# A two-layer latent diffusion backbone on one core: statistics of the Fourier mixer on TensorE, and five changes to the order of small steps

## The chip, the cores and the metric

The kernel runs on one core of a Trainium2 chip. A core has five engines that run side by side, each with its own instruction queue: TensorE (PE in the profile; its weight loads are PEld), VectorE (DVE), ScalarE (ACT), GpSimd (POOL) and SyncE (SP), which here issues most DMAs. The metric is the device time of one execution in microseconds; below, the time of a kernel is the median of its runs.

## What is computed

Two layers over 512 tokens of 1024 channels, all in fp32. The first layer's mixer is attention, the second's is a Fourier mix; each layer ends with a gated feed-forward net (FFN) with a width-3 convolution over tokens. Cut to what matters here:

```python
for i in range(2):
    sh1, sc1, g1, sh2, sc2, g2 = split(silu(c) @ mod_w[i] + mod_b[i])      # "adaLN"
    h = rms_norm(x, norm_g[i, 0]) * (1 + sc1) + sh1
    if i == 0:
        y = attention_mixers(h, ...)
    else:
        y = real(fft2(h in 4 channel groups)) @ w_f
    x = x + g1 * rms_norm(y, norm_g[i, 1])
    h = rms_norm(x, norm_g[i, 2]) * (1 + sc2) + sh2
    u = conv3(h @ w_up)                       # 2 x 2816 columns: gate and value
    y = (silu(gate) * value) @ w_down
    x = x + g2 * rms_norm(y, norm_g[i, 3])
```

Every rms_norm needs the sum of squares over all 1024 channels of a token.

## The kernel before, in words

Activations lie with channels on the 128 partitions: 8 tiles of 128 channels by 512 tokens, in two halves of 256 tokens. An fp32 operand is split into a high and a low part, and each product is three matmuls (`mm3`, L108 to L110: high times high, high times low, low times high). So each weight tile needs a cast on ACT and a subtraction on DVE (`split`, L144); up to five such pairs are held at a time (`wpair`), and three raw tiles.

A scheduler places the instructions of each engine in an order fixed before the run: an instruction becomes a candidate when its inputs and buffers are ready in the scheduler's own clock, and among candidates the one written first goes first. Three helpers bind the order by hand: `follow(i, j)` puts i behind j on their engine, `in_turn` chains whole steps on PE and DVE, and `fence()` with `held()` keeps weight splits (and the adaLN sums) behind what was written before the fence. `later(n)` makes a step count as written n places later. At run time each engine works through its own queue in order.

The places that the change touches, in order of time:

- **adaLN sums in layer 0's FFN** (`gemv_jobs`, L538 on; from 323 to 632 us). Five vectors of 1024 outputs are made on DVE: eight multiply-adds of 1024 columns into `gacc` (L570, L573), then `gemv_end` sums over partitions by four 32-column matmuls (L615), copies, transposes (L625) and adds the bias. The generator is pumped one step at a time between FFN tiles.
- **The Fourier mix** (`over_tokens`, `cosines`, `sines`, `group`, then the loop over d at the end of that section). For each of 8 output tiles d, an odd part (12 matmuls with B) and an even part (15 matmuls, the first three with N, the rest with A) make `yT[:, d]`: ACT copies the odd part to `qs`, DVE adds for columns 0 to 255 (L1923), ACT copies column 256 (L1926), DVE subtracts for the rest (L1927). ACT squares the tile (L316), POOL adds the squares of d = 1 to 5 into `acc` (L318; L305 writes the first), those of d = 6 and 7 go to TensorE directly, and ACT scales the tile by its gate (L1933). TensorE sums squares over partitions by `stat_add` (L211): four 32-column matmuls of 64 tokens each for a half. DVE also makes the sum and difference of the next `w_f` tile (L1833, L1834) and its low part. Meanwhile POOL issues DMAs that load the second FFN's first four weight tiles and add their low parts to ACT's `wl = -wh` (L1325 to L1335).
- **The second FFN's opening.** Five first up-projections (units) run over half 0, then half 1; `remod` (L351 on) writes the final input of a half, tile by tile, on DVE and ACT. The sixth unit runs half 0, then half 1.
- **Units by seven products.** From f = 8 on in layer 1 (and for ten f in layer 0) an up-projection pair is made by a Strassen-like scheme of seven products of half size (`seven_products`, L1379 on). `seven_inputs` (L1346 on) makes the combined inputs, eight DVE operations of 1024 columns and four casts; for layer 1 it stands ahead of f = 7. Three copies on ACT (L1398, L1400, L1402) take partial products out of PSUM; the later products of the unit write where these copies read. The weights of the next unit are cast on ACT too; the cast of "1", 512 columns, needs only the raw tile's DMA.
- **The last adaLN vector** (`gemv_pair`), pumped at the down-projection tiles that GEMV lists for each group.
- **The end** (L1947 on). Half 1 of the last down-projection ends tile by tile: DVE adds (L1487), ACT squares (POOL adds up five of them, L318; the last three stay apart, L309), ACT scales by the gate (L1949). `sums_all` sums the four squares over partitions (L226), and `rstd_all` makes 1/sqrt by an ACT estimate `r` (L232), `v` = mean + eps (ACT, L233) and three DVE steps (L234 to L236).

## Time and profile before

| what | us |
|---|---|
| median of 3 runs | 1095.69 (1092.93 to 1097.57) |
| the profiled execution, its own time | 1092.73 |
| the profiled span | 1091.0 |

In the profile a line such as "L144 ACT CAST wh<-raw" is one instruction or a group of them: line of the kernel, engine, operation, written tile and read tiles. "[0.59 <-DVE gacc L573]" behind an instruction says that its engine sat idle for 0.59 us before it and which instruction the profile takes to have ended that. Matmuls overlap: a 256-column one is shown 0.28 us long while the next starts 0.11 us after it. The granted TensorE clock was 1.00 in every stretch that was asked for.

### The profile page before, as it was taken

What the parts mean: (1) busy time and instruction counts of PE and PEld (TensorE: products, weight loads), DVE (VectorE), ACT (ScalarE), POOL (GpSimd) and SP (SyncE); (2) the same over time, 40 slices, a digit from 0 to 9 for tenths busy, and PEclk for the clock granted to TensorE, in tenths of its full rate; (3) what the DMA queues carried; (4) which work ended last, traced back from release to release, by engine and by line L of the source; (5) the groups of instructions that cost most, each with busy time, mean ns of one, the idle gap of its engine ahead of it and who ended that gap; (6) DMA issues with size and microseconds to landing.
All of it is one profiled execution on the core that took longest, in us unless ns stands there. A gap on an engine that the chain in (4) does not pass through costs nothing.

```text
span 1091.0 us, 22506 instructions
## 1 busy us (share of the span) xinstructions
PE 1067.9 (98%) x9352; PEld 1006.0 (92%) x9352; DVE 890.3 (82%) x1451; ACT 601.5 (55%) x1060; POOL 112.3 (10%) x119
## 2 busy tenths in 40 slices
PE   9999999999999999999999999999999999999997
PEld 5699888869999999999999999979999999999996
DVE  5788877774679976878999877888998999889855
ACT  4442366675656633552465476767755465556533
POOL 0046122522100000000000020310000000000012
PEclk9999999999999999999999999999999999999999
DMA  9776101175231474426724630842215533323342
GB/s 367 284 261 213 40 1 40 37 270 196 78 156 39 157 261 147 171 88 229 263 84 153 228 108 2 261 126 117 90 38 169 200 107 114 115 86 103 113 149 78
DMA packets 33911, 156.53 MB, mean 143 GB/s; under 512 B 3472, under 2 KB 8208, under 8 KB 22160
## 3 DMA queue, kind: packets, MB, share of 16 engines
q1 hardware_dynamic: 32656, 150.89, 38.6%
q0 software_dynamic: 1152, 4.19, 1.6%
q8 instruction: 73, 1.20, 0.4%
q14 instruction: 30, 0.25, 0.1%
HBM read 148.78 MB, written 6.29 MB: 142 GB/s over the span
## 4 chain that ended last, share of the span: by engine, by line
PE 72%; DVE 16%; ACT 5%; DMA 3%; issue 3%; POOL 0%; DVEq 0%; POOLq 0%; SPq 0%; ACTq 0%
PE mm L108 20%; PE mm L110 19%; PE mm L109 19%; DVE wl L144 4%; PE PT L1123 1%; DVE cv L1462 1%; DVE cv L1464 1%; ACT wh L144 1%; DMA xl<-in_mod_r 1%; PE gm L108 1%; ACT yT L366 1%; PE O L109 1%; PE gm L109 1%; PE gm L110 1%; PE O L108 1%
## 5 line engine op out<-in xcount | busy, mean ns | idle before, releaser
L144 ACT CAST wh<-raw 128x1024 fp32r<-128x1024 f32 (+2 forms) x206 | 189.9, 931 | 150.6 <-PE mm L109 92.3
L108 PE MATMUL mm<-hh,wh 128*128 128x256 f32 x852 | 236.8, 279 | 3.3 <-ACT sq L1400 2.6
L144 DVE TENSOR_TENSOR wl<-raw,wh 128x1024 fp32r<-128x1024 f32 (+2 forms) x206 | 219.7, 1072 | 23.3 <-ACT wh L144 22.4
L110 PE MATMUL mm<-hh,wl 128*128 128x256 f32 x852 | 235.4, 277 | 1.4 <-DVE wl L144 1.4
L109 PE MATMUL mm<-hl,wh 128*128 128x256 f32 x852 | 235.7, 277 | 0.3 <-DVE hl L369 0.3
L108 PEld LDWEIGHTS mm<-hh,wh 128*128 128x128 f32 x852 | 159.7, 188 | 5.7 <-ACT sq L1400 3.0
L110 PEld LDWEIGHTS mm<-hh,wl 128*128 128x128 f32 x852 | 160.1, 188 | 2.4 <-DVE wl L144 2.3
L109 PEld LDWEIGHTS mm<-hl,wh 128*128 128x128 f32 x852 | 159.9, 188 | 0.6 <-DVE hl L369 0.5
L108 PE MATMUL mm<-xh,wh 128*128 128x256 f32 x492 | 136.7, 279 | 0.0
L109 PE MATMUL mm<-xl,wh 128*128 128x256 f32 x492 | 136.3, 277 | 0.0
L110 PE MATMUL mm<-xh,wl 128*128 128x256 f32 x492 | 135.9, 277 | 0.0
L108 PE MATMUL mm<-zh,wh 128*128 128x256 f32 x384 | 106.6, 278 | 0.5 <-ACT sq L1398 0.5
L110 PE MATMUL mm<-zh,wl 128*128 128x256 f32 x384 | 106.2, 276 | 0.0
L109 PE MATMUL mm<-zl,wh 128*128 128x256 f32 x384 | 106.2, 276 | 0.0
L108 PEld LDWEIGHTS mm<-xh,wh 128*128 128x128 f32 x492 | 92.3, 188 | 1.3 <-issue 0.4
L109 PEld LDWEIGHTS mm<-xl,wh 128*128 128x128 f32 x492 | 92.4, 188 | 0.5 <-issue 0.4
L110 PEld LDWEIGHTS mm<-xh,wl 128*128 128x128 f32 x492 | 92.4, 188 | 0.0
L318 POOL TENSOR_TENSOR cv<-cv,sq 128x256 f32<-128x256 f32 x20 | 16.6, 832 | 702.0 <-ACT sq L316 702.0
L108 PEld LDWEIGHTS mm<-zh,wh 128*128 128x128 f32 x384 | 72.1, 188 | 1.1 <-ACT sq L1398 0.9
L110 PEld LDWEIGHTS mm<-zh,wl 128*128 128x128 f32 x384 | 72.2, 188 | 0.0
L109 PEld LDWEIGHTS mm<-zl,wh 128*128 128x128 f32 x384 | 72.1, 188 | 0.0
L1461 ACT ACTIVATE cv<-mm,cols 128x512 f32<-128x512 f32 x59 | 45.7, 776 | 12.8 <-DVE mm L1405 7.9
(472 smaller groups left out, 2789.8 us busy)
## 6 DMA issues: line engine op xcount, KB each, us to landing
raw<-in_w_up SPq DMA_DIRECT2D x42, 1024.0 KB, 5.0
xT<-in_mod_r SPq DMA_DIRECT2D x20, 1024.0 KB, 4.9
raw<-in_w_down SPq DMA_DIRECT2D x32, 384.0 KB, 3.1
raw<-in_mod_p SPq DMA_DIRECT2D x8, 1024.0 KB, 5.0
raw<-in_w_down SPq DMA_DIRECT2D x16, 512.0 KB, 4.8
raw<-in_w_in SPq DMA_DIRECT2D x6, 1024.0 KB, 8.3
yT<-in_mod_r SPq DMA_DIRECT2D x10, 512.0 KB, 5.9
raw<-in_w_out SPq DMA_DIRECT2D x4, 1024.0 KB, 5.8
```

Source lines behind the costliest of these rows:

```text
L108: i = PE.matmul(out, lhsT=ah, rhs=bh, start=start, stop=False, skip_group_check=skip)
L109: PE.matmul(out, lhsT=ah, rhs=bl, start=False, stop=False, skip_group_check=skip)
L110: return i, PE.matmul(out, lhsT=al, rhs=bh, start=False, stop=stop, skip_group_check=skip)
L144: i = S.copy(out=h, in_=src), eng.tensor_tensor(out=l, in0=src, in1=f(h), op=ALU.subtract)
L318: G.tensor_tensor(out=self.acc[:, sl], in0=self.acc[:, sl], in1=sq[:, sl], op=ALU.add)
L366: S.activation(out=yT[:, c, halves[h]], in_=yT[:, c, halves[h]], func=AF.Identity, bias=bm[:, c:c + 1], scale=am[:, c:c + 1])
L1123: PE.transpose(out=pt[:, j * P:(j + 1) * P], in_=Ps[j][:, off:off + P], identity=ident)
L1461: S.activation(out=cv, in_=ps, func=AF.Identity, bias=bc, scale=wc[1])
L1462: V.scalar_tensor_tensor(out=cv[:, 1:], in0=ps[:, :T - 1], scalar=wc[0], in1=cv[:, 1:], op0=ALU.mult, op1=ALU.add)
L1464: V.scalar_tensor_tensor(out=cv[:, :T - 1], in0=ps[:, 1:], scalar=wc[2], in1=cv[:, :T - 1], op0=ALU.mult, op1=ALU.add)
```

## The change

It moves the sums of squares of the Fourier loop from POOL to TensorE (`RowSums`, with `run` behind the even part of d = 2, 4 and 6), fixes the order of that loop's steps on PE, folds column 256 into the DVE addition and puts N last in the even part; takes the last token block's sines ahead of its cosines and lets the fence stand ahead of the last `cosines`; gates of d = 0 to 5 count as written 1000 places later, those of 6 and 7 come by halves behind the last square. In the FFNs: the end of adaLN jobs 2 to 4 comes one pump later, and for jobs 3 and 4 its matmuls are bound behind the PE instruction written last; `gemv_pair` is spread over three groups; `seven_inputs` of layer 1 is written behind f = 7; the sixth unit's two halves are parted by the first half of the next unit, whose gate weights are cast ahead of `remod(1)` and whose value weights stay behind a new fence; the cast of "1" must follow the copy L1402 of the unit before. At the end, the last three gates follow the last square, the sums run in the order sixth tile, seventh, `acc`, eighth, each bound behind the one before, and `v` is made on DVE.

```diff
-GEMV = {0: (0, 5, 7), 1: (0, 2, 4, 6)}
+GEMV = {0: (0, 7), 1: (1, 3, 5), 2: (0, 2)}
+GAP = 2
...
 def rstd_all(ps):
-        S.activation(out=v, in_=ps, func=AF.Identity, bias=eps, scale=1.0 / D)
+        V.tensor_scalar(out=v, in0=ps, scalar1=1.0 / D, scalar2=EPS, op0=ALU.mult, op1=ALU.add)
...
 def sums_all(self, pps, h):
-            stat_all(ps, self.acc[:, halves[h]], True, False)
-            for sq in self.last[h]:
-                j = stat_all(ps, sq[:, halves[h]], False, sq is self.last[h][-1])
+            a, b, c = self.last[h]
+            sq, j = [a, b, self.acc, c], []
+            for i, s in enumerate(sq):
+                j.append(stat_all(ps, s[:, halves[h]], i == 0, s is c))
+                if i:
+                    follow(j[i], j[i - 1])
...
+    class RowSums:
+        def square(self, src, d, hs):
+            if d not in self.sqs:
+                self.sqs[d] = self.sq = mk(cp, [P, T], F32, "sq", 2)
+            sl = slice(hs[0] * HT, (hs[-1] + 1) * HT)
+            self.end = S.activation(out=self.sqs[d][:, sl], in_=src[:, sl], func=AF.Square)
+        def run(self, ds, hs=(0, 1)):
+            for h in hs:
+                for d in ds:
+                    stat_add(self.ps[h], self.sqs[d][:, halves[h]], HT, d == 0, d == KC - 1)
...
 def gemv_jobs(jobs, pps, away=None):
             end = gemv_end(l, v, acc, pps)
-            next(end)
+            if places and job == GAP:
+                yield
+            if places and job > GAP:
+                behind_pe(end)
+            else:
+                next(end)
...
 def seven_weights(l, fi):
-            split(wh, wl, src)
+            c = split(wh, wl, src)[0]
+            if names == "1" and copied:
+                follow(c, copied.pop())
 def seven_products(l, fi, pps, bs):
-        S.copy(out=xs[:, HT:], in_=y[:, HT:])
+        copied.append(S.copy(out=xs[:, HT:], in_=y[:, HT:]))
...
 def ffn(l, xp, ready, pre, mid, gem, plain=None):
+            ahead = up_weights(l, wpair, [FIRST])
+            wa = next(ahead)
             remod(1, *n2, R[1])
+            fence()
+            wa = [wa, next(ahead)]
...
-                for s in halves:
-                    up_mm(ps, w, s)
+                m = [up_mm(ps, w, halves[0])]
+                pa = mk(pps, [P, T], F32, "mm", 6)
+                m += [up_mm(pa, wa[0], halves[0]), up_mm(ps, w, halves[1])]
+                for j in (1, 2):
+                    follow(m[j][0][0], m[j - 1][-1][1])
...
-                if fi == SUMS[l]:
+                if fi == SUMS[l] and fi in SEVEN[l]:
                     bs = seven_inputs(xp)
...
+                    if fi == SUMS[l]:
+                        bs = seven_inputs(xp)
...
 # the Fourier section
+        for g in range(4):
+            in_turn(sines, g, [3])
         for g in range(4):
             in_turn(group, g, [3])
+        fence()
         in_turn(cosines, None, [v[:4] for v in N], [z[:, :, :, P] for z in Z], list(range(TT)), True)
-        fence()
...
-        ys = YStat(wk, 2)
+        turn.pop(mybir.EngineType.DVE)
+        ys = RowSums(pps)
...
-                pump(soon)
+                with later(60):
+                    pump(soon)
...
+            in_turn(odd, d, wh, wl)
+            pp = in_turn(even, d, wh, wl)
+            if d in (2, 4, 6):
+                in_turn(ys.run, [d - 2, d - 1])
+            qs = qq[d % 2]
+            V.tensor_tensor(out=yT[:, d, 0:257], in0=pp[:, 0:257], in1=qs[:, 0:257], op=ALU.add)
             if d == KC - 1:
-                ys.add(pps, yT[:, d, halves[0]], [0])
-            S.copy(out=yT[:, d, 256:257], in_=pp[:, 256:257])
+                in_turn(ys.run, [d - 1])
+                ys.square(yT[:, d, :], d, [0])
+                in_turn(ys.run, [d], [0])
             V.tensor_tensor(out=yT[:, d, 511:256:-1], in0=pp[:, 1:256], in1=qs[:, 1:256], op=ALU.subtract)
+            ys.square(yT[:, d, :], d, [1] if d == KC - 1 else [0, 1])
             if d == KC - 1:
-                ys.add(pps, yT[:, d, halves[1]], [1])
-            else:
-                ys.add(pps, yT[:, d, :], [0, 1])
-            with later(3000 if d == KC - 1 else 0):
-                S.activation(out=yT[:, d, :], in_=yT[:, d, :], func=AF.Copy, scale=der[:, 1, 1, d:d + 1])
+                in_turn(ys.run, [d], [1])
+            if d < 6:
+                with later(1000):
+                    gate(d, slice(0, T))
+        with later(3000):
+            for hs in halves:
+                for d in (6, 7):
+                    follow(gate(d, hs), ys.end)
...
 # the end
-            S.activation(out=yT[:, k, hb], in_=yT[:, k, hb], func=AF.Copy, scale=der[:, 1, 3, k:k + 1])
+            j = S.activation(out=yT[:, k, hb], in_=yT[:, k, hb], func=AF.Copy, scale=der[:, 1, 3, k:k + 1])
+            if k > KC - 4:
+                follow(j, ys.square)
```

The even part now runs A first and N last; `odd` writes the copied odd part into one of two fixed tiles whose column 256 is zero.

More of the change, by code (lines that the diff above doesn't have):

```diff
@@ L308, in add @@
                 sq = mk(self.late, [P, T], F32, "cv%d" % (n % 2), 2)
-                S.activation(out=sq[:, sl], in_=src, func=AF.Square)
+                self.square = S.activation(out=sq[:, sl], in_=src, func=AF.Square)
                 self.last[1].append(sq)
@@ L324, in sums_all @@
             ps = mk(pps, [P, T], F32, "misc", 2)
-            stat_all(ps, self.acc[:, halves[h]], True, False)
-            for sq in self.last[h]:
-                j = stat_all(ps, sq[:, halves[h]], False, sq is self.last[h][-1])
-            return ps, j
+            a, b, c = self.last[h]
[4 more added lines that the diff above has]
+                    follow(j[i], j[i - 1])
+            return ps, j[-1]
         def sums(self, pps, h):
@@ L337, in sums, with __init__ @@
             self.last = {0: [], 1: []}
+            return self.ps[h]
+    class RowSums:
+        def __init__(self, pps):
+            self.ps = [mk(pps, [P, T], F32, "misc", 2) for _ in halves]
+            self.sqs = {}
+        def square(self, src, d, hs):
[7 more added lines that the diff above has]
+                    stat_add(self.ps[h], self.sqs[d][:, halves[h]], HT, d == 0, d == KC - 1)
+        def sums(self, pps, h):
             return self.ps[h]
@@ L559, in gemv_jobs @@
         n = 0
-        for l, v in jobs:
+        for job, (l, v) in enumerate(jobs):
             acc = mk(cp, [P, D], F32, "gacc", 1)
@@ L1358, in seven_inputs @@
         return b
+    copied = []
     def seven_weights(l, fi):
@@ L1627, in ffn @@
                     cc = []
-                    for i, w in enumerate(up_weights(l, wpair, [fi])):
-                        ps = mk(pps, [P, T], F32, "mm", 6)
-                        m = [up_mm(ps, w, s) for s in halves]
-                        follow(m[1][0][0], m[0][-1][1])
+                    given = l and fi == FIRST
+                    for i, w in enumerate(wa if given else up_weights(l, wpair, [fi])):
+                        if given and i == 0:
+                            ps = pa
+                            up_mm(ps, w, halves[1])
+                        else:
+                            ps = mk(pps, [P, T], F32, "mm", 6)
+                            m = [up_mm(ps, w, s) for s in halves]
+                            follow(m[1][0][0], m[0][-1][1])
                         cc.append(conv(fi, i, ps))
+                    if fi == SUMS[l]:
+                        bs = seven_inputs(xp)
                 gated(fi, cc[0], cc[1], f0)
@@ L1822, in group @@
         def group(g, ts):
-            if ts[-1] == TT - 1:
-                sines(g, ts)
             cosines(g, [v[:, g, :] for v in A], [z[:, :, g, 0:P] for z in Z], ts)
@@ L1905, with odd, even, gate @@
         soon = up_weights_dma(1, xp.weights, [0, 1])
-        ys = YStat(wk, 2)
+        turn.pop(mybir.EngineType.DVE)
+        ys = RowSums(pps)
+        qq = [mk(wk, [P, 258], F32, "qs%d" % i) for i in range(2)]
+        for q in qq:
+            V.memset(q[:, 256:257], 0.0)
+        def odd(d, wh, wl):
+            pq = mk(pps, [P, T], F32, "mm", 6)
+            for g in range(4):
+                mm3(pq[:, :256], wh[:, 1, g, :], wl[:, 1, g, :], B[0][:, g, :], B[1][:, g, :], g == 0, g == 3)
+            S.copy(out=qq[d % 2][:, :256], in_=pq[:, :256])
+        def even(d, wh, wl):
+            pp = mk(pps, [P, T], F32, "mm", 6)
+            for g in range(4):
+                mm3(pp[:, :M1], wh[:, 0, g, :], wl[:, 0, g, :], A[0][:, g, :], A[1][:, g, :], g == 0, False)
+            mm3(pp[:, :M1], nyh[:, d * P:(d + 1) * P], nyl[:, d * P:(d + 1) * P], N[0], N[1], False, True)
+            return pp
+        def gate(d, hs):
+            return S.activation(out=yT[:, d, hs], in_=yT[:, d, hs], func=AF.Copy, scale=der[:, 1, 1, d:d + 1])
         for d in range(KC):
```

10 lines of the change are left out of this document (removed).

## The prediction

> **What bounds the kernel now.** I read the page first, then the chain of waits that ended last, then each engine's waits, then a table by stretches of time, then the timeline around every stop of TensorE.
>
> ```profile
> span 1091.0 us, 22506 instructions
> ```
>
> ```profile
> PE 1067.9 (98%) x9352; PEld 1006.0 (92%) x9352; DVE 890.3 (82%) x1451; ACT 601.5 (55%) x1060; POOL 112.3 (10%) x119
> ```
>
> The profiled execution took 1092.73 us in all, 1.73 beyond this span; the median of the runs is 1095.69, 2.96 above it. TensorE is the bound, and what can be won is its stops. The next view gives stretches: start and end, length, busy time of PE, PEld, DVE, ACT and POOL, then clock and DMA share.
>
> ```profile
> 520.00:580.00 60.00, 59.25 (x519) 58.08 (x518) 58.42 (x72) 32.29 (x51) 0.00 (x0) 1.00 0.48 169
> 690.00:720.00 30.00, 27.38 (x249) 26.16 (x247) 25.04 (x40) 22.28 (x44) 13.41 (x13) 1.00 0.99 297
> 755.00:824.00 69.00, 68.01 (x595) 67.56 (x594) 67.80 (x103) 47.29 (x71) 0.00 (x0) 1.00 0.19 63
> 849.00:927.00 78.00, 75.44 (x664) 74.51 (x663) 75.52 (x97) 45.20 (x72) 0.00 (x0) 1.00 0.38 129
> ```
>
> In three of them DVE is as full as PE (58.42 of 60, 67.80 of 69, 75.52 of 78 us): a stop removed there can come back as a wait for DVE. In the Fourier loop (690 to 720) the DMA engines are full instead (0.99). Now TensorE's stops that the change touches, from the timeline; the bracket is the idle time before the instruction and what ended it.
>
> ```profile
> 513.04 0.64 PE L615 MATMUL misc<-gacc,ones 128*32 128x256 f32 x8 [0.59 <-DVE gacc L573]
> 544.33 0.39 PE L110 MATMUL mm<-hh,wl 128*128 128x256 f32 x1 [0.41 <-DVE wl L144]
> 575.12 0.38 PE L110 MATMUL mm<-hh,wl 128*128 128x256 f32 x1 [0.31 <-DVE wl L144]
> 691.23 0.39 PE L109 MATMUL mm<-B,wh 128*128 128x256 f32 x1 [0.39 <-DVE B L144]
> 692.79 0.39 PE L108 MATMUL mm<-N,wh 128*128 128x258 f32 x1 [0.72 <-ACT N L144]
> 714.57 0.38 PE L108 MATMUL mm<-B,wh 128*128 128x256 f32 x1 [0.43 <-ACT yT L1926]
> 715.83 0.38 PE L110 MATMUL mm<-B,wl 128*128 128x256 f32 x1 [0.76 <-DVE wl L144]
> 762.16 0.38 PE L109 MATMUL mm<-hl,wh 128*128 128x256 f32 x1 [0.34 <-DVE hl L369]
> 808.98 0.38 PE L110 MATMUL mm<-hh,wl 128*128 128x256 f32 x1 [0.64 <-DVE wl L144]
> 866.35 0.39 PE L108 MATMUL mm<-hh,wh 128*128 128x256 f32 x1 [1.56 <-ACT sq L1400]
> 881.22 0.38 PE L108 MATMUL mm<-hh,wh 128*128 128x256 f32 x1 [0.99 <-ACT sq L1400]
> ```
>
> A stop costs more than its bracket. The rows below (of the second FFN's opening, where squares are already summed on TensorE) show why, and price such a sum as well.
>
> ```profile
> 729.36 0.28 PE L109 MATMUL mm<-hl,xh 128*128 128x258 f32 x1
> 729.48 0.28 PE L110 MATMUL mm<-hh,xl 128*128 128x258 f32 x1
> 729.69 0.43 PE L211 MATMUL mm<-yT,ones 128*32 128x64 f32 x16
> 730.05 0.39 PE L108 MATMUL mm<-hh,xh 128*128 128x258 f32 x1
> 730.28 0.29 PE L109 MATMUL mm<-hl,xh 128*128 128x258 f32 x1
> ```
>
> Matmuls start 0.12 us apart but are drawn 0.28 long, so 0.16 of a stop hides under the drawn end; and the first one after it holds up the next by 0.23 instead of 0.12. So a stop costs its bracket plus about 0.28.
>
> **The change, part by part.**
>
> *adaLN sums later.* PE waits 0.59 + 0.28 = 0.87 us at 513 for `gacc`; a pump later the sum is long made. Two further stops follow, 0.41 and 0.31 plus 0.28 each, 1.28 together, where weights' low parts come late from a full DVE. Of job 3 the last two multiply-adds, 1.28 us each by the row below, move behind them.
>
> ```profile
> L573 DVE SCALAR_TENSOR_TENSOR gacc<-xT,cols,gacc x35: 1272/1276/1287, 372.9 to 613.0; 128x1024 f32<-128x1024 f32 x35
> ```
>
> They are 2.56 us of DVE against 1.28 of stops, but job 3 also begins a pump later, and if DVE idles meanwhile, that wastes what was won. Between all and nothing I take half: -0.6. The restore of `xT` and job 4's sums move by one pump too, where PE sees no stop. Part: -1.5 (-0.9 to -2.2).
>
> *Fourier loop, entry.* The stops at 691.23 and 692.79 cost 0.67 and 1.00. With all sines first, B is split early and the first goes. For N:
>
> ```profile
> 692.77 0.41 DVE L144 TENSOR_TENSOR N<-mm,N 4x258 fp32r<-4x258 f32 x1 [0.60 <-ACT N L144]
> ```
>
> N's low part is done at 693.18, last of a chain on DVE that the change doesn't shorten. Its use moves behind 12 matmuls with A, 12 x 0.12 = 1.44 us, but PE gets there 0.67 earlier: wanted at 691.92 - 0.67 + 1.44 = 692.69, one matmul later for the low part. About 0.5 us of waiting stays. Entry: -1.67 + 0.5.
>
> *Fourier loop, POOL.* The stops at 714.57 and 715.83 cost 0.71 and 1.04. Both follow the last weight tile, whose sum and difference DVE makes late:
>
> ```profile
> 693.71 0.67 DVE L1834 TENSOR_TENSOR gacc<-raw 128x512 f32<-128x512 f32 x1
> 711.21 2.23 DVE L1834 TENSOR_TENSOR gacc<-raw 128x512 f32<-128x512 f32 x1
> L318 POOL TENSOR_TENSOR acc<-acc,sq x5: 1288/1573/1746, 700.5 to 717.0; 128x512 f32<-128x512 f32 x5
> ```
>
> The same operation takes 0.67 alone and 2.23 in the stretch in which POOL adds squares. Without those five additions I count the stops as gone: -1.75.
>
> *Fourier loop, TensorE's new work.* Before, six sums of a tile's half (`acc` and two squares, twice) ran at the loop's end, where PE waited anyway. Now there are 16, of which 12 stand in three bursts of four inside the loop. Two squares cost, by the rows at 729, 730.28 - 729.48 less two normal starts of 0.12: 0.56 us. The 16 small matmuls' own time, 0.43 less a drawn end of 0.28, doubles in a burst of four, which makes 0.7 at least; twice 0.56, 1.1, is the most. I take 0.8: +2.4 (2.1 to 3.4). [...]
>
> *Fourier loop, squares.* A burst stands on PE behind the even part of d and needs the square of d - 1; behind a burst that waits stand all products. One even part, the late case:
>
> ```profile
> 710.68 0.28 PE L110 MATMUL mm<-A,wl 128*128 128x258 f32 x1
> 716.20 0.63 ACT L316 ACTIVATE sq<-yT 128x512 f32<-128x512 f32 x1 [1.35 <-DVE yT L1927]
> ```
>
> Tile 5's products end at 710.8 and its square at 716.83, 6 us later; PE needs 27 x 0.12 = 3.2 us to the next burst. Before, nobody waited for that. The change takes away what made it late: POOL's additions, the wait of the subtraction for the copy of column 256, and gates ahead of squares. I take 0.5 in all (0 to 3 x 2.8). The tail (add, square, sum, 1/sqrt, spread, first update) keeps its steps; column 256 no longer parts its add and subtraction, but half 1 is not what the opening waits for. Loop with entry: -1.67 + 0.5 - 1.75 + 2.4 + 0.5 = 0.0 (-1.3 to +9).
>
> *Second FFN opens on the next unit.* The stop at 762.16 costs 0.62; 24 matmuls, 2.9 us, now lie ahead of it. The stop at 808.98 costs 0.92: PE waits for f = 7's weights behind `seven_inputs` on DVE, and these now come after. DVE then still has 67.80 us to do in 69.00 - 1.54 = 67.46, so I let 0.3 return: -1.2 (0 to -1.5).
>
> *Copies ahead of casts.* PE's two longest stops, 1.84 and 1.27 us, wait for a copy that ACT could have made earlier:
>
> ```profile
> 865.41 0.62 ACT L144 CAST wh<-raw 128x512 fp32r<-128x512 f32 x1 [2.53 <-DMA raw<-in_w_up]
> 865.93 0.37 ACT L1400 COPY sq<-mm 128x256 f32<-128x256 f32 x1
> ```
>
> ACT sits 2.53 us before a cast whose raw tile is still under way, and the copy stands behind it; so it is before the other stop. That 512-column cast is "1", and bound behind L1402 it can't stand there. Delayed, it is still made before the unit's last four products end (48 matmuls, 5.8 us). DVE has 75.52 us for 78 - 3.1; one pair of `gemv_pair`'s multiply-adds leaves the stretch, so I let 0.3 return: -2.8 (-2.2 to -3.1). The moved `gemv_pair` steps fall to stretches where PE has no stop; its DMAs wait on SP for DVE's reads as before.
>
> *The end.*
>
> ```profile
> DVE st_v L218 <- ACT st_r L217: 19.0, 10, 8.7
> 1079.36 0.51 ACT L1949 ACTIVATE yT<-yT,der 128x256 f32<-128x256 f32 x1
> 1079.78 0.40 ACT L309 ACTIVATE cv<-yT 128x256 f32<-128x256 f32 x1
> 1078.84 2.08 PE L226 MATMUL misc<-cv,ones 128*128 128x256 f32 x8 [0.35 <-POOL cv L318]
> 1081.53 0.43 DVE L234 TENSOR_TENSOR md_t<-md_t 128x256 f32<-128x256 f32 x1 [2.58 <-ACT md_t L232]
> 1082.07 0.43 DVE L235 SCALAR_TENSOR_TENSOR md_t<-md_t,md_t 128x256 f32<-128x256 f32 x1
> ```
>
> The last square ends at 1080.18, 0.74 us before the sums do. Two of the gates stand ahead of squares; without them the square can come up to 0.8 earlier. But the eight sums, 2.08 us with their waits, gain at their start only the 0.35 that POOL's `acc` cost, so I take -0.5. Against it, `v` moves to DVE. In the helper that does so already, DVE waits for ACT's `r` each time (the first row: 19.0 us, 10 times), though `v` doesn't use `r`. Here `v` now runs beside on ACT and costs 0.11 (1081.96 to 1082.07); behind `r` it stands ahead of L234 with some 0.4: +0.3. [...] Part: -0.2.
>
> Sum: -1.5 + 0.0 - 1.2 - 2.8 - 0.2 = -5.7. Made against the profiled execution it gives 1087.0; against the median, which is what will be measured, **1090.0 us**. About 0.5% (5.5 us) is what a measurement of this kernel can tell from no change, so the forecast lies on that edge.
>
> **The rivals.**
>
> *DVE gives the waits back.* In the three full stretches only stops that ACT or order caused go for good: 0.87 at 513, about 2.4 of the copies, 0.2 at the end. Then -3.5: 1092.2. For it: 58.42, 67.80 and 75.52. Against it: DVE has slack after each (82% overall).
>
> *The Fourier loop loses.* Bursts at 1.1 and squares late by 0.9 each time: +3.0 there, -2.7 in all: 1093.0.
>
> *Slower.* Each burst waits as long as tile 5's square would make it, 2.8 us, and costs 1.1: the loop loses 9, and the sum is +3.3: 1099.0. It decides from a square that ends more than 3.2 us behind its even part; a net loss needs 5.7 of such waits. Beside it stands the last low part of the early weights:
>
> ```profile
> L1335 POOL DMA_DIRECT2D xl<-in_w_up x1: 867/867/867, 710.7 to 710.7; - x1
> DMA to landing us min/median/max: 10.2/10.2/10.2
> 724.58 0.40 PE L1529 MATMUL mm<-hh,xh 128*128 128x258 f32 x1 [0.53 <-ACT hh L490]
> ```
>
> It landed at 720.9, 3.7 us ahead of the opening; `later(60)` puts the ACT step ahead of it later, and beyond 3.7 the opening waits.
>
> *Nothing returns.* Every stop above goes and the bursts stay at 0.7: -2.2 - 1.3 - 1.5 - 3.1 - 0.5 = -8.6: 1087.1.
>
> **How the numbers follow.** Forecast 0.44, DVE 0.16, loop loses 0.14, slower 0.08, nothing returns 0.18. Half of the forecast lies beyond 0.5%, and nearly all of the last: 0.24 + 0.18 + 0.02 = 0.44 faster. Of the slower rival most stays within 0.5%; with the late weights 0.06. The rest, 0.50, is the same. The range runs from the best case less the half-spread of three runs (2.3 us), 1084.5 rounded, to the middle of the slower one's, 1097.5.
>
> **What would show it.** Right: no stop before an L108 for ACT's L1400; ACT's 512-column cast behind L1402; DVE's L1834 at 0.67 throughout; none at 762 and 809; DVE's `v` behind L232. Wrong: a stop before L211 in the loop for ACT's square; a wait of L1529 or L1530 for a DMA into `xl`; DVE above 98% with new stops for `wl`.

## The result, and the profile after

The changed kernel takes 1105.42 us (median of 6 runs, 1102.98 to 1114.1) beside 1094.88 us of the kernel before (6 runs, 1091.44 to 1097.57): a ratio of 1.0114 with a 95% interval of 1.0088 to 1.014. It is 1.1% slower, clear of the noise; the forecast was 1090.0, and its range ended at 1097.5. The profiled execution after took 1107.07 us. Its page, by engine:

```profile
span 1105.3 us, 22661 instructions
```

```profile
PE 1075.8 (97%) x9432; PEld 1013.0 (92%) x9432; DVE 889.8 (81%) x1454; ACT 600.8 (54%) x1053; POOL 105.4 (10%) x114
```

PE's idle time rose from 23.1 us (1091.0 less 1067.9) to 29.5; its busy time rose by 7.9. The 80 matmuls more, small ones of which 32 take 0.65 us, can't fill that, so PE was also slower while it was busy. To find the place, both traces are cut at the same points of the work: the end of layer 0's FFN, the end of the Fourier loop, then the first, eighth and fifteenth product of the units of the second FFN. Columns are start and end, length, busy time and instructions of PE, PEld, DVE, ACT and POOL, granted clock, DMA share and GB/s. Before:

```profile
501.02:660.65 159.63, 158.22 (x1449) 154.86 (x1447) 141.71 (x201) 86.44 (x146) 8.78 (x10) 1.00 0.50 177
660.65:742.54 81.89, 78.04 (x820) 71.97 (x821) 68.37 (x142) 54.13 (x116) 13.41 (x13) 1.00 0.46 142
742.54:771.09 28.55, 28.21 (x263) 27.40 (x263) 24.80 (x56) 24.55 (x44) 0.00 (x0) 1.00 0.28 112
771.09:823.26 52.17, 51.53 (x455) 51.33 (x453) 51.88 (x74) 31.22 (x44) 0.00 (x0) 1.00 0.19 60
823.26:939.00 115.74, 113.18 (x997) 112.25 (x996) 104.04 (x132) 66.29 (x106) 0.00 (x0) 1.00 0.42 142
```

And after:

```profile
501.97:671.95 169.98, 161.58 (x1449) 157.64 (x1447) 143.15 (x201) 86.62 (x146) 9.62 (x10) 0.98 0.45 166
671.95:753.13 81.18, 79.24 (x900) 73.22 (x901) 64.78 (x144) 53.98 (x110) 5.92 (x8) 1.00 0.46 144
753.13:780.24 27.11, 27.11 (x254) 26.47 (x254) 22.58 (x54) 22.84 (x42) 0.00 (x0) 1.00 0.26 100
780.24:838.74 58.50, 54.42 (x463) 54.04 (x462) 54.44 (x76) 33.49 (x46) 0.00 (x0) 0.97 0.18 63
838.74:952.04 113.30, 112.16 (x989) 111.96 (x988) 104.15 (x132) 65.56 (x105) 0.00 (x0) 1.00 0.43 144
```

Below, these are "the end of layer 0", "the Fourier mix", "the opening", "units to the eighth" and "units to the fifteenth". The differences are +10.35, -0.71, -1.44, +6.33 and -2.44; what lies before is +0.95, and the rest of the products and the end +1.10 and +0.16. Together they make 14.30, as the spans do. So two stretches lose 16.7 us, and of the five shown they alone have a clock below 1.00. The cut between the opening and units to the eighth goes by DVE's first product. At that point PE has done 9 matmuls less after than before (254 beside 263 in the opening, 463 beside 455 behind it), so 1.0 us of the -1.44 and of the +6.33 is only work on the other side of the cut.

*The end of layer 0.* Its timeline in the trace of before, on DVE: job 3's last step, then the first and the last multiply-add of job 4 (the five jobs are counted from 0).

```profile
577.72 0.15 DVE L627 TENSOR_TENSOR mods<-misc,cols 128x8 f32<-128x8 f32 x1
578.45 0.74 DVE L570 TENSOR_SCALAR gacc<-xT,cols 128x1024 f32<-128x1024 f32 x1
612.99 1.28 DVE L573 SCALAR_TENSOR_TENSOR gacc<-xT,cols,gacc 128x1024 f32<-128x1024 f32 x1
```

The same steps after, with what follows from them on SP, ACT and PE:

```profile
615.68 0.17 DVE L657 TENSOR_TENSOR mods<-misc,cols 128x8 f32<-128x8 f32 x1 [3.14 <-PE misc L655]
615.76 0.74 DVE L595 TENSOR_SCALAR gacc<-xT,cols 128x1024 f32<-128x1024 f32 x1
...
630.16 0.94 ACT L145 CAST zh<-raw 128x896 fp32r<-128x896 f32 x1 [1.77 <-DMA raw<-in_w_down]
630.32 1.27 DVE L598 SCALAR_TENSOR_TENSOR gacc<-xT,cols,gacc 128x1024 f32<-128x1024 f32 x1
...
631.15 0.58 PE L109 MATMUL mm<-xh,zh 128*128 128x256 f32 x1 [3.98 <-ACT zh L145]
```

The one pump by which job 3's end moved is 38 us long here (577.72 to 615.68). No run parts the pump from the bond of job 3's sums behind PE; in the trace ACT's copy of these sums is done at 596.2, 19 us ahead of the transposes (615.3), which carry no bond, so it isn't the bond that holds them there. Job 4 needs the same `gacc`, so its eight multiply-adds, spread over 36 us before, are crowded into 16 us, among the splits of the last down projection's weights. The chain of waits shows what that does (start, length, what):

```profile
620.81 0.72 DVE gacc L598
...
622.61 1.15 DVE wl L145
623.77 6.36 DMA raw<-in_w_down
...
```

DVE first stood idle for 3.14 us in front of job 3's last step, which waited for PE's transposes; job 4's first step came behind it, at 615.76. Then multiply-adds stand ahead of a weight's low part; the low part frees a raw tile at 623.76; only then does SP issue the next load, at 623.77; it lands 6.36 us later, and PE stops for 3.98 us. That stop is followed by another mechanism, which the stretches of time show:

```profile
630.34:633.75 3.41, 2.60 (x12) 2.60 (x13) 3.41 (x5) 0.96 (x2) 0.00 (x0) 0.50 0.57 183
633.75:637.17 3.42, 3.42 (x22) 2.80 (x21) 0.55 (x3) 0.00 (x0) 0.00 (x0) 0.50 0.94 350
...
790.74:794.15 3.41, 3.06 (x14) 3.06 (x15) 3.41 (x7) 1.25 (x2) 0.00 (x0) 0.50 0.00 0
```

The granted clock is 0.50 for 6.8 us behind this stop and for 3.4 us in the second FFN; matmuls then start 0.21 us apart instead of 0.11. Three further stops of this stretch are 2.02 us at 543 (for ACT's `sq`), 0.91 at 575 and 1.42 at 647 (both for `wl`). The one at 543 is job 3's too: the chain of waits leads back from the copy to a multiply-add at 539.86 that waited 1.41 us for its load. The four stops with 0.28 each and half of the 6.02 us in which PE was busy at the slow clock make 12.5, and the stops of before that went were worth 2.15: +10.3 worked out, +10.35 measured.

*Units to the eighth.* PE's stops there, after:

```profile
788.00 0.36 PE L109 MATMUL mm<-hh,wh 128*128 128x256 f32 x1 [1.45 <-DVE cv L1498]
...
791.10 0.58 PE L111 MATMUL mm<-hh,wl 128*128 128x256 f32 x1 [2.62 <-DVE wl L145]
```

Two stops, 4.63 us with 0.28 each, and half of the 3.06 us that PE was busy at the slow clock; 0.92 of before went: +5.2, beside +5.3 measured (6.33 less the 1.0 us of the cut). The low part waited for is late because of DVE's order:

```profile
774.91 0.68 DVE L394 TENSOR_TENSOR hl<-yT,hh 128x512 fp32r<-128x512 f32 x1
...
789.83 1.22 DVE L145 TENSOR_TENSOR wl<-raw,wh 128x1024 fp32r<-128x1024 f32 x1
```

The first row is the last step of `remod`, the last row is the first low part of f = 4. Between them the convolutions of the first units (L1494 to L1509) stand on DVE. Counting DVE's instructions in the traces, those that only wait among them, f = 4's two low parts are the 38th and 44th behind the last `hl` after, and the corresponding two were the 15th and 19th before. Whether the new fence does this or the moved `seven_inputs` was not to be seen in the profile.

### The profile page after: what moved, and what is told of

Read it like the earlier page. It is cut to its first block, busy times and chain, and to the rows that moved or that the text cites. A ratio compares the mean times of both kernels' runs of the same rounds, so it can differ in the third digit from the quotient of the medians.

```text
span 1105.3 us, 22661 instructions
## 1 busy us (share of the span) xinstructions
PE 1075.8 (97%) x9432; PEld 1013.0 (92%) x9432; DVE 889.8 (81%) x1454; ACT 600.8 (54%) x1053; POOL 105.4 (10%) x114
## 4 chain that ended last, share of the span: by engine, by line
PE 80%; DVE 9%; ACT 5%; DMA 3%; issue 2%; POOL 0%; DVEq 0%; SPq 0%; ACTq 0%; POOLq 0%
PE mm L109 22%; PE mm L111 22%; PE mm L110 22%; DVE wl L145 2%; PE PT L1153 1%; DMA xT<-in_mod_r 1%; DVE gacc L598 1%; ACT yT L391 1%; PE gm L109 1%; PE O L110 1%; ACT wh L145 1%; PE gm L110 1%; PE gm L111 1%; PE misc L212 1%; PE O L109 1%
```

## The experiments

The first theory was: two places lose time, independently; the adaLN step costs some 10 us and the new fence some 5, the rest gains a little. The rivals were that the moved `seven_inputs` causes the second loss, and that the clock's fall, not the late weights, makes the first. Ratios are to the kernel before on the same chip, with 95% intervals.

**adaLN's ends back.**

```diff
-            if places and job == GAP:
-                yield
-            if places and job > GAP:
-                behind_pe(end)
-            else:
-                next(end)
+            next(end)
```

> The changed kernel with its adaLN edit undone (no extra step, sums as before); all else stays changed. Theory A: the extra step makes job 3's transposes come at 615 instead of 578 us, job 4's eight multiply-adds wait for them (one gacc buffer), and their loads into xT stand on SP ahead of the last down projection's weights; TensorE then stops 4.0 us and its clock halves. Undone, the delay that opens between 598 and 642 us (about 10.6 us) goes: 1095 us (1093 to 1097), no stop over 1 us and clock 1.00 between 600 and 650. Rival: the end of layer 0 was so full already that the other edits (the copies bound ahead of casts change ACT's order there too) cause most of it; then at most 4 us return: 1101 or more, and a stop for the down weights stays.

It took 1098.18 us, 1.0056 [1.0038, 1.0074]. This is the end of layer 0, then units to the eighth:

```profile
501.74:661.69 159.95, 159.00 (x1449) 156.01 (x1447) 142.17 (x201) 86.51 (x146) 8.80 (x10) 1.00 0.49 176
...
770.05:829.10 59.05, 54.43 (x460) 54.05 (x460) 54.45 (x76) 33.47 (x46) 0.00 (x0) 0.94 0.19 64
```

The end of layer 0 is back at 159.95 with the clock at 1.00: the step costs 10.0 there. The second loss stays whole, with 6.8 us of slow clock in place of 3.4. The time came out 3 us above what was expected.

**The fence alone taken out.** `fence()` behind `remod(1, *n2, R[1])` is dropped, so that the splits of f = 4 are no longer held behind it.

```diff
             remod(1, *n2, R[1])
-            fence()
```

> The changed kernel without the one fence written behind remod(1); the opening on the next unit's first half and the later seven_inputs stay. Theory F: the fence keeps unit f = 3's second split behind remod(1), so its raw tile stays taken and f = 4's load is issued at 777.4 us; in the kernel before it was issued at the equivalent of 774, and f = 4's low parts come 18 DVE instructions later. Without the fence the two stops of 1.5 and 2.6 us at 786 and 788 and the half-clock stretch behind them go: 6 us return, 1099.5 (1098 to 1101). Rival: TensorE arrives there earlier and DVE is simply full with the convolutions of the opening, whatever their order; then stops of 3 us or more stay between 780 and 800 and the time stays above 1103.

It took 1100.21 us, 1.0069 [1.0047, 1.0091]. The opening, then units to the eighth:

```profile
753.08:782.51 29.43, 27.80 (x262) 27.05 (x262) 25.80 (x57) 25.33 (x45) 0.00 (x0) 1.00 0.29 109
782.51:834.72 52.21, 52.00 (x458) 51.81 (x458) 50.70 (x74) 30.33 (x43) 0.00 (x0) 1.00 0.18 61
```

58.50 became 52.21, as before the change (52.17), and f = 4's low parts are the 16th and 17th behind the last `hl`. But the opening lost its gain (29.43 beside 27.11): PE now waits 1.63 us for a convolution's step before it gets a PSUM buffer. So the fence gains 2.3 in one stretch and costs 6.3 in the next, 4.0 on balance. The account of raw tiles and loads in this expectation fell: the load that it goes by is that of f = 6. A later experiment tests the order on DVE instead.

**`seven_inputs` back ahead of f = 7**, with all else as changed.

```diff
-                if fi == SUMS[l] and fi in SEVEN[l]:
+                if fi == SUMS[l]:
...
-                    if fi == SUMS[l]:
-                        bs = seven_inputs(xp)
```

> The changed kernel with seven_inputs of layer 1 written ahead of f = 7 again; the opening and its fence stay. Theory F (the fence): f = 4's low parts stay 29 DVE instructions behind the last hl, so the stops at 786 to 791 stay and the time is 1105 within 2, or a little above (the old stop at 809 may return, 0.9). Rival: moving seven_inputs changed DVE's order and caused the stops; then 6 us return: 1099.5.

It took 1108.87 us, 1.0141 [1.0114, 1.0167]. Units to the eighth took 60.98 at a clock of 0.94, with stops of 2.02 and 2.62 us. This rival falls: the place of `seven_inputs` isn't what makes the low parts late.

**Both losses mended.** The version without the fence, and adaLN's jobs 3 and 4 as before; only job 2's end keeps its later place, which had removed the stop at 513.

```diff
             if places and job == GAP:
                 yield
-            if places and job > GAP:
-                behind_pe(end)
-            else:
-                next(end)
-            yield
+            next(end)
+            if not places or job != GAP:
+                yield
...
-            fence()
```

> The changed kernel with two repairs: no fence behind remod(1), and job 2's sums one step later without pushing what follows (its transposes share the step, jobs 3 and 4 stand as in the kernel before). If theories A and F hold and add up, 10.6 and 6 us return and the stop at 513 stays away: 1088 to 1091, against 1094.9 for the kernel before, so 0.4 to 0.6% faster. If instead part of the loss belongs to the Fourier loop or the copies, it stays at or above 1093.

It took 1093.37 us (12 runs), 1.0012 [0.9994, 1.003]: level with before, and 2 us above the expected span of times. The expectation's alternative, that part of the loss belongs to the Fourier loop or the copies, fits the time but not the stretches: the mix took 81.63 and units to the fifteenth 112.06, both less than before, and the end of layer 0 161.69 with stops of 0.42 and 0.51 us; PE was busy there 2.28 us longer than before the change (160.50 beside 158.22), with as many matmuls and the clock at 1.00, and the last section tells of such a slower pace. So what the change loses is in these two places, and what it was to gain elsewhere does not show in the time. The next runs go after that.

**Mended, with the opening as before** (the early weights, the sixth unit's order and `seven_inputs` all back).

```diff
-            ahead = up_weights(l, wpair, [FIRST])
-            wa = next(ahead)
             remod(1, *n2, R[1])
-            wa = [wa, next(ahead)]
...
```

> The repaired kernel (job 2's sums later without pushing what follows) with the opening as in the kernel before: no interleaved half of the next unit, seven_inputs ahead of f = 7. In the repaired kernel the stretch from the second store of xT to the first product of the second FFN takes 29.43 us against 28.55 in the kernel before, with a new stop of 1.63 us at 762.7 behind L1492, which frees a PSUM buffer. Theory P: the half that is taken ahead needs a seventh mm buffer where six exist, so the opening itself loses 0.9 even without the fence; undone, that stretch is back at 28.5 and the time is 1092.5. Rival (my forecast): the opening is worth 1.2, the wait for the buffer would come anyway; then 1094.5.

1095.2 us (12 runs), 1.0012 [0.9991, 1.0033]. The opening took 28.55, as said, and stops of 0.34, 0.63 and 1.31 us are back at 762, 808 and 878. The opening's edits are worth 0 within the interval.

**Mended, without the bond of the cast of "1" to the copy.**

```diff
-            if names == "1" and copied:
-                follow(c, copied.pop())
```

> The repaired kernel without the bond of the cast of 1 behind the copy L1402. Theory: the bond takes away the stops of 1.57 and 0.99 us for L1400 that the kernel before shows at 864.5 and 880.0; without it they return, the stretch from unit 29 to unit 36 takes 2.0 to 2.6 us more (114.5), 1095.5 in all. Rival: they went because gemv_pair's multiply-adds left that stretch; then the stretch stays at 112.1 to 112.6.

1094.46 us (10 runs), 1.0013 [0.999, 1.0036]. Units to the fifteenth took 114.52 as expected, but for another reason: no stop for the copies was above 0.3 us, and PE was busy 2.55 us longer than in the mended version (114.41 beside 111.86), which fits the slower pace of the last section. The number was right and the theory behind it wrong.

**Mended, with the old places of `gemv_pair`.**

```diff
-GEMV = {0: (0, 7), 1: (1, 3, 5), 2: (0, 2)}
+GEMV = {0: (0, 5, 7), 1: (0, 2, 4, 6)}
```

> The repaired kernel with gemv_pair pumped as before (two groups). Theory: spreading it moves 1.1 us of its sums and transposes from the stretch of units 29 to 36 into the one behind it and is worth nothing by itself: the first stretch takes 1.1 more (113.2), the second 1.1 less (139.5), the time stays 1093.4 within 1.5. Rival: with its multiply-adds back, DVE is full there and the stops for copies or low parts return: 2 us or more, 1095.5.

1093.56 us (10 runs), 0.9996 [0.9976, 1.0016]. Units to the fifteenth 113.09 instead of 112.06, the rest of the products 139.52 instead of 140.62: 1.1 us move from one stretch to the other, and nothing is won.

**Mended, with neither bond nor new places** (both edits above together).

> The repaired kernel without the fence, with gemv_pair pumped as before and without the bond of the cast of 1: of the changes to the FFN of layer 1 only the opening and the later seven_inputs are left. Without the bond alone, and with the old gemv_pair alone, the stretch of units 29 to 36 stayed 2.7 to 3.4 us (net of pace) under the 115.75 of the kernel before; with the old opening it rose by 2.3. Theory: the stops for the copy L1400 went because of the opening, not the bond: the stretch stays at 113.0 to 113.6 at the fast pace. Rival: the bond or the spread gemv_pair is enough by itself, and with neither the stops of 1.6 and 1.0 return: 115.5.

1090.64 us (10 runs), 0.9965 [0.9949, 0.9982]. Units to the fifteenth took 114.67, between the two theories, with stops of 1.08 and 0.72 us for the copies. One profile of each can't rank the edits: the largest stop of this stretch is 0.51 us with the bond alone, below 0.3 with the new places alone, and anything from none to 1.56 us in the nine profiles that have both.

**The kernel before once more**, as a kernel of its own, with no edit, to see how far one profile of it speaks for the next.

> The kernel before, unchanged, profiled a second time. Undisturbed matmuls of 256 columns start either 0.113 or 0.118 us apart, for tens of us at a time; between 308 and 501 us, where all these kernels run the same instructions, the profiles so far differ by up to 4 us in this. Theory: the pace isn't set by the program but by chance at the last stop: this profile has its slow stretches elsewhere than the first (430 to 478 us) and its span differs by 1 us or more through them alone. Rival: the pace follows from the order of the program; then the same stretches are slow and the spans agree within 0.5. Time 1093.4 within 2 either way.

1092.04 us (10 runs), 0.9985 [0.9967, 1.0004]. The two stops for the copies, 1.56 and 0.99 in the profile on which the prediction rests, were here:

```profile
865.96 0.39 PE L108 MATMUL mm<-hh,wh 128*128 128x256 f32 x1 [0.48 <-ACT sq L1400]
...
880.12 0.39 PE L108 MATMUL mm<-hh,wh 128*128 128x256 f32 x1 [0.28 <-ACT sq L1400]
```

Units to the fifteenth took 113.96 instead of 115.74. In the first profile each of these copies stands behind a cast that waited for a DMA, 2.53 and 1.76 us, and the stops differ by 1.08 and 0.71 us between two executions of one program; -2.8 was read from a bad one. On the pace the theory held by half: the slow stretches lie elsewhere (see the last section), but the span is 1.1 us shorter, with 1.8 us less in this stretch, while the same work kept PE busy 0.90 us longer at the end of layer 0 (159.12 beside 158.22).

**The fence kept, f = 4's splits earlier.** adaLN as in the mended version; with the fence in place, f = 4's splits count as written 120 places earlier (`sooner` wraps each split in `later(-n)`).

```diff
...
-                    for i, w in enumerate(wa if given else up_weights(l, wpair, [fi])):
+                    for i, w in enumerate(wa if given else sooner(up_weights(l, wpair, [fi]), 120 if l and fi in (4,) else 0)):
```

> The changed kernel with job 2's sums repaired, the fence behind remod(1) kept, and only the splits of unit f = 4 counted as written 120 places earlier, so that its two low parts stand 8 and 5 DVE instructions further ahead. My account of the fence by f = 3's raw tile was wrong: the load at 777.4 us is f = 6's, f = 4's tile had long landed and its casts on ACT were done at 778.2; what is late is its low part on DVE (789.8). Theory D: the fence hurts through DVE's order alone; then the stop of 2.6 us for the low part goes, the clock stays 1.00, and the stretch from unit 22 to unit 29 falls from 58.5 to 53.5 to 55 (a wait of 1.5 for a PSUM buffer stays): 1094.5. Rival: DVE is simply full; then the wait moves to the next buffer or low part, the sum of stops between 780 and 800 stays above 3 us and the stretch above 56.5.

1091.4 us (10 runs), 0.997 [0.9949, 0.999]. The two low parts are now the 28th and 37th behind the last `hl` instead of the 38th and 44th. The opening, then units to the eighth:

```profile
742.92:770.04 27.12, 27.12 (x257) 26.48 (x257) 22.59 (x54) 22.84 (x42) 0.00 (x0) 1.00 0.25 98
770.04:824.27 54.23, 53.17 (x466) 52.78 (x466) 53.98 (x76) 33.22 (x46) 0.00 (x0) 1.00 0.20 68
```

PE's stops in them are 0.91 and 0.15 us, the clock stays at 1.00, and the opening keeps its 27.12. Units to the eighth get 4.3 us back by the order alone: the late low parts on DVE cause the loss, and the fence sets that order. The stops left make 1.06 us, beside 0.98 in the same two stretches before the change (0.34 and 0.64), so the opening still wins nothing.

**Mended, with `seven_inputs` ahead of f = 7** (the diff of the third experiment, on the mended version).

> The repaired kernel without the fence, with seven_inputs of layer 1 ahead of f = 7 again and the opening on the next unit's half kept. It parts the two halves of the opening's edit. Theory: the interleaved half alone costs the 0.9 at 762.7, and seven_inputs behind f = 7 alone takes away the stop of 0.64 at 809 and shifts the later copies: here the stretch to unit 22 stays 29.4, that of units 22 to 29 rises by 0.6 to 0.9 (52.9), that of units 29 to 36 by up to 2.3 (114.3): 1095. Rival: it is the interleaved half that shifts what follows; then both later stretches stay at 52.2 and 112.1.

1091.66 us (10 runs), 0.9985 [0.9954, 1.0015]. Units to the eighth 52.29 beside 52.19: the move of `seven_inputs` is worth nothing there. Units to the fifteenth took 115.38; PE was busy there 1.96 us longer than in the mended version (113.82 beside 111.86), and a stop of 1.56 us at 877 came back; this run doesn't decide more.

**The stop in layer 0 filled.** The changed kernel, with 34 matmuls that nobody reads in PE's 4-us stop at 627 (bound behind the matmuls ahead of the stop), so that PE isn't idle there while the weights are as late as ever.

```diff
...
+                    if d == 4:
+                        fp = mk(pps, [P, T], F32, "mm", 6)
+                        for n in range(34):
+                            j = PE.matmul(fp[:, :HT], lhsT=ws[3][0][0], rhs=g_[0][0][:, :HT], start=True, stop=True)
...
```

> The changed kernel with 34 matmuls of 128x256 that nobody reads put into TensorE's stop of 4.0 us at 627 (behind the first two matmuls of down tile d = 4, ahead of d = 5; they add work and leave none out). They take 34 x 0.113 = 3.85 us. Theory: the half clock from 630.3 to 637.2 follows from the stop; filled, the clock stays 1.00 and the 26 matmuls behind it start 0.113 apart instead of 0.214: 2.7 us less, 1102.7. Rival: the halving has another cause (the load of the DMA engines, 0.94 there, or what DVE and ACT do); then the matmuls stay 0.214 apart and the time is 1105.4 or up to 0.5 more.

1111.12 us (4 runs), 1.015 [1.0102, 1.0198]. Its PE timeline at the fill and 17 us later:

```profile
627.17 4.02 PE L1735 MATMUL mm<-xh,wh 128*128 128x256 f32 x34
...
644.67 0.39 PE L109 MATMUL mm<-xh,wh 128*128 128x256 f32 x1 [2.03 <-ACT wh L145]
```

and its stretches behind the fill and behind the new stop:

```profile
630.00:634.00 4.00, 4.00 (x39) 3.86 (x41) 4.00 (x5) 0.26 (x2) 0.00 (x0) 1.00 0.55 172
646.50:650.00 3.50, 3.50 (x19) 3.50 (x18) 2.65 (x4) 1.69 (x4) 1.15 (x1) 0.52 0.45 151
```

With PE busy the clock stays at 1.00 from 630 to 634, where it was 0.50 from 630.34 on in the changed kernel, so there it was PE's idle time that lowered it. But the end of layer 0 took 170.39 us, as in the changed kernel (169.98): PE ran ahead and stopped 2.03 us for the next cast, and the clock fell there. So the rival of another cause falls, and so does the gain of 2.7 that the theory expected: the 10 us are set by the chain of low part, raw tile and load, and the slow clock lay inside that chain. The time lies above what either expected; in its profile units to the eighth take 1.1 us more than in the changed kernel, with 6.8 us of slow clock instead of 3.4, and the rest of the products 2.1 more, at the slower pace (PE busy 142.69 beside 140.55).

## Why the prediction was wrong, point by point

*adaLN sums later (forecast -1.5, measured +10.35): the step that decides.* It failed at "The restore of `xT` and job 4's sums move by one pump too, where PE sees no stop." The stop at 513 went, as said. But a pump was taken for a small shift, and it is 38 us at this place; job 4 cannot start before `gacc` is read; and its work on DVE then stands ahead of the low parts whose end frees the raw tiles. The prediction had named DVE's idling as a risk, but priced it at half of 1.28 us; DVE stood idle for 3.14 us at one step. What counted was not whether PE stops there now, but what stands behind each moved instruction in its queue. Undone, it gives 10.0 back.

*Second FFN opens on the next unit (forecast -1.2, measured -1.44 and +6.33).* It failed at "so I let 0.3 return". The stops at 762 and 809 went, as said, and 0.4 of the -1.44 is left when the cut is allowed for. But this needs the fence, and the fence was counted as free. It orders DVE so that f = 4's low parts come 22 and 27 instructions later than without it. The earlier splits brought 4.3 of it back. The rival that DVE gives the waits back had the engine and the stretch, but its price came from DVE's busy share; order, not load, was the cause (DVE's busy time from the opening through the eighth product rose by only 0.3 us, from 76.68 to 77.02). The sign "DVE above 98% with new stops for `wl`" came by half: stops of 0.91, 1.42 and 2.62 us for `wl` are new, with DVE at 93% in units to the eighth (54.44 of 58.50).

*A stop priced at its bracket and 0.28.* Behind single stops up to 1.63 us (with both losses mended) the clock stayed at 1.00. Those of 2.0 us and more, the one at 543 apart, brought 3.4 or 6.8 us of half clock as well, which no term of the sum had; the prediction noted a clock of 1.00 and asked no further.

*Copies ahead of casts (forecast -2.8, measured -2.44 in this pair of profiles).* The agreement is chance. The prediction took it that with the 512-column cast gone from there, nothing keeps the copy waiting. In the changed kernel other steps do. ACT, then PE:

```profile
891.31 0.64 ACT L1508 ACTIVATE cv<-cv 128x512 f32<-128x512 f32 x1 [0.80 <-DVE cv L1498]
892.53 0.82 ACT L145 CAST wh<-raw 128x768 fp32r<-128x768 f32 x1
893.25 0.38 ACT L1432 COPY sq<-mm 128x256 f32<-128x256 f32 x1
893.68 0.39 PE L109 MATMUL mm<-zh,wh 128*128 128x256 f32 x1 [1.14 <-ACT sq L1432]
```

L1432 is the copy that was L1400. It now stands behind the convolution's steps and a 768-column cast, and PE still stops for it, 1.14 us here and 1.31 to 1.56 in three other versions with the bond. So the first sign of being right did not come. Against the second profile of before, the stretch gained 0.66, and the mended version without the bond ran level with the one that has it. With the 1.1 us of `gemv_pair`, which the prediction took to fall where PE has no stop and which cost just as much there, the two edits together bring nothing that these runs can measure. The size came from one execution's stop, which was taken for the kernel's.

*Fourier loop (forecast 0.0, measured -0.71).* The mix takes 81.15 to 81.63 us in the changed kernel and every version of it, beside 81.89 and 81.74 in the two profiles of before. A burst in the trace after:

```profile
711.21 0.28 PE L111 MATMUL mm<-N,wl 128*128 128x258 f32 x1
711.42 0.65 PE L212 MATMUL misc<-sq,ones 128*32 128x64 f32 x32
712.00 0.39 PE L109 MATMUL mm<-B,wh 128*128 128x256 f32 x1
712.23 0.28 PE L110 MATMUL mm<-B,wh 128*128 128x256 f32 x1
```

From 711.21 to 712.23 are 1.02 us; less two normal starts of 0.12, the burst costs 0.78, beside 0.8 forecast. None of the three bursts inside the loop waited for a square, where 0.5 was allowed (PE's idle time in the mix is 1.93 or 1.94 us in the changed kernel and in each of its versions); the last sum behind the loop waits 0.68 us for its square, where 0.51 stood before. N still costs a wait: from the last product with A to the first of the next odd part (703.85 to 704.96) PE takes 0.63 more than four normal starts, beside 0.5. DVE's sum and difference fell to their price without POOL. The group (count, busy, mean ns) before and after:

```profile
L1834 DVE TENSOR_TENSOR gacc<-raw 128x512 f32<-128x512 f32 x4 | 4.3, 1064 | 0.0
```

```profile
L1880 DVE TENSOR_TENSOR gacc<-raw 128x512 f32<-128x512 f32 x4 | 2.7, 683 | 0.0
```

With no burst inside the loop waiting, the mechanism of the two rivals in which the loop loses did not occur.

*The end (forecast -0.2, measured +0.16).* `v` behind `r` costs what was said:

```profile
1095.62 0.42 DVE L234 TENSOR_SCALAR md_t<-misc 128x256 f32<-128x256 f32 x1 [2.53 <-ACT md_t L233]
1095.96 0.41 DVE L235 TENSOR_TENSOR md_t<-md_t 128x256 f32<-128x256 f32 x1
```

0.34 us from the one start to the next, +0.3 forecast. The -0.5 of earlier squares wasn't there: from the last tile's addition to this step it is 2.95 us, and was 3.00. The last square did come earlier, 0.58 us behind that addition instead of 1.25, but the eight sums then took 2.27 us instead of 2.08.

*The slower rival* had the right sign, but not the size (1099.0 beside 1105.42), and its mechanism did not occur. What happened stood in no rival: a wait that an edit makes for weights, by order on DVE.

What stays open: of the parts that gained in the stretches (the Fourier mix, the opening, units to the fifteenth), no version shows more than 0.35% in the time. The version with neither bond nor new places and the one with the fence and earlier splits are fastest, 0.9965 and 0.997, and the kernel before against itself gave 0.9985 in the same set; by that measure they are ahead by 0.1 to 0.2%, which these runs can't tell from nothing.

## What to carry to other kernels

When a step is moved in the program, ask how long the move is in time at that place and what stands behind the step in its engine's queue; a full buffer, a late low part and a load that is issued only when a buffer is free turn steps of 1.3 us into a 4-us stop. A fence that is added for one order sets all the others behind it too, so read the position of the next weights on DVE, not DVE's busy share. When one step is taken from ahead of another, look which step stands there next. And take the size of a stop that hangs on a DMA from more than one execution.

## What the runs showed of the hardware that was not expected

*The clock falls behind short stops.* In the changed kernel it fell behind a stop of 3.98 us and behind two of 1.45 and 2.62 us that stood some 0.5 us of work apart. In the version without the fence it fell behind stops of 2.54 and 0.39 us (627.9 to 631.4), and only at 632.5, when PE was at work again; with `seven_inputs` back, behind 2.16 and 0.62 us; with the stop filled, behind 2.03 and 0.76 us. Stops of 1.56 us in the kernel before (866.35) and of 1.63 us with both losses mended (764.58) lowered nothing, and neither did the 2.02 us at 543 in the changed kernel. These falls lasted 3.4 or 6.8 us each, and in the changed kernel the clock changes at 630.34, 637.16, 790.76 and 794.18 us, which are 2, 45 and 1 steps of 3.413 us apart. Cut into these steps, the changed kernel shows (length, then busy time of PE; the clock stands third from the end):

```profile
541.59:545.00 3.41, 1.73 (x16) 1.53 (x14) 3.41 (x5) 2.25 (x4) 0.00 (x0) 1.00 0.27 50
545.00:548.42 3.42, 3.08 (x27) 3.09 (x28) 3.42 (x5) 0.93 (x4) 0.00 (x0) 1.00 0.61 256
...
626.92:630.34 3.42, 0.25 (x3) 0.05 (x1) 3.42 (x5) 1.62 (x5) 2.06 (x2) 1.00 0.28 107
```

The stop at 543 leaves 1.68 us of idle time in its step, and the clock stays; the one at 627 leaves 3.17, and the clock is 0.50 from 630.34 on. The profiles of the changed kernel and of the versions with adaLN's ends back, without the fence, with `seven_inputs` back and with the stop filled show eight falls behind 500 us and ahead of the end; the 3.41 us ahead of each have 1.76 to 3.17 us of idle time (1.76 without the fence, 629.09 to 632.50). In the kernel before, 1.70 us of it between 1084.00 and 1087.42 lowered nothing. So the idle time within a step fits these falls better than the length of one stop; eight falls are too few to read a limit from, and what the clock goes by was not shown.

*Matmuls have two paces at the same clock.* This is an undisturbed stretch of 20 us in the profile of before:

```profile
340.00:360.00 20.00, 20.00 (x179) 20.00 (x178) 20.00 (x25) 11.87 (x18) 0.00 (x0) 1.00 0.20 63
```

and the same stretch in the second profile of the same program:

```profile
340.00:360.00 20.00, 20.00 (x172) 20.00 (x171) 19.95 (x24) 12.36 (x18) 0.00 (x0) 1.00 0.21 66
```

The same matmuls start 0.113 us apart (179 in 20 us) or 0.118 (172), PE busy throughout and the clock at 1.00 in both; at 445 to 465 the two profiles have it the other way round, 172 and 179. In the trace of before the pace changes behind a stop of 0.59 us at 319, in that of after at 310 behind a burst of small matmuls without a stop, and there it then holds at 0.118 until 416; which one comes was different for the same program. Summed over an execution the slower pace cost 5.3 us before (1198 matmuls of 256 columns at 0.1178 instead of 0.1133 us) and 7.3 after (1641), as much as the edits in dispute, so stretches of two profiles are compared only where both have the same pace. What sets it was not found.
